# Issuing a gated recurrence and its projections in a written order on one Trainium2 core

## The chip, the cores and the metric

The kernel runs on one core of one Trainium2 chip. A core has a tensor engine (PE, matrix products and transposes), a vector engine (DVE), a scalar engine (ACT, activations and copies), GpSimd (POOL) and a sync engine (SP) that issues most DMAs. Each engine works through its own list of instructions in the order of that list, and engines wait for each other by semaphores. The metric is the device time of one execution in microseconds.

## The reference

One step of a streaming encoder with one layer: 512 prompt frames and 32 frames of a running stream, model width 2048, all in float32. Half of the token mixer is latent attention, half is a gated linear recurrence (HGRN2) with 8 heads of 128 features. The stage that is changed computes the recurrence:

```python
proj = x @ w_in
hq, hf, hi, hg, cq, ckv, kr = jnp.split(proj, SPLITS, axis=-1)
f = lb + (1.0 - lb) * jax.nn.sigmoid(hf)
# S_t = diag(f_t) S_{t-1} + k_t outer v_t (k_t = 1 - f_t), o_t = S_t^T q_t
o_h, s_new = hgrn2_recurrence(heads(hq), heads(1.0 - f), heads(jnp.log(f)), heads(hi), s0, blk)
o_h = rms_norm(o_h, hgrn_norm_g) * jax.nn.silu(hg)
...
out = jnp.concatenate([o_h, o_a], axis=-1) @ w_out
```

Behind it come a normalisation, a convolutional feed-forward network and a last normalisation.

## The kernel before

Activations lie with features on the 128 partitions and all 544 frames along the free axis. Each float32 operand of a large product is split into a high part (`wh` of a weight, `aH` of an activation, rounded by ACT) and a low part (`wl`, `aL`: what the rounding left, subtracted by DVE), and a product is three matmuls: high by high, high by low, low by high.

**The projections of heads 2 to 7** are made by one step of Strassen's scheme over halves of the frames and of the input features. A *group* makes two projections of a head, `divided_qf(h)` the query q and the forget gate f, `divided_ig(h)` the value i and the output gate g. Each group is seven *products*, in the order 11, s1, s2, s4, s3, 12, 22. A product is 24 matmuls with 272 columns, eight blocks of features by three (L753). Its weight is a quarter matrix of 128x1024 or a difference of quarters: `form` (L711, DVE) makes the difference for s1, s2, s3 and 22, `split` (L717 on ACT, L718 on DVE) makes wh and wl. Products 11, 12 and s4 take a loaded quarter as it is; `form("11")` issues the four loads of a group. When a product ends, its result is copied by ACT (L759) or added by DVE (L762) into the projection's tile `hproj`, and the gate's function follows (sigmoid on ACT; L774 or L784 on DVE).

**The recurrence of a head** runs beside these products. `levels(h)` has nine steps: Kp = 1 - f and Qp = q*f (L801, L802); the diagonal term (dps, L807) with level 1; levels 2, 4, 8, 16, 32, 64, each with four or five small matmuls of Kp by Qp (L822, L824, L827), an update of Qp on DVE (L828), one of Kp on POOL (L830), and a masked copy of the scores into `attnT` (L840); at last a record of the tiles. Each level's matmuls read Kp and Qp as the level before left them. `finish(h)` makes the head's outputs: transposes of Kp and of the value (L856) into one PSUM tile `sw`, copied by ACT to kT (L858, L859) and vT (L861); the state products (L866) and the states S on DVE (L871, L873); the output matmuls (L888, L890); their square on ACT (L893); its sum and a scaling on DVE (L896, L897); a power on POOL (L898); the product with it on DVE (L900); the transposes of that (L906), again in `sw`; and the scaling by the gate (L908, L910).

**The order.** `weave` lets the levels of head h run beside `divided_ig(h)`, and the outputs of head h beside `divided_qf(h+1)`, by a ratio of steps. This only sets priorities: the scheduler that builds each engine's list chooses among what it holds to be ready. `ready(n + 2)` has the weights of the product two ahead formed and split. Elsewhere the kernel uses `tc.manual_schedule(engines=MANUAL)`, under which PE, DVE and ACT get their instructions in the order in which the code issues them; POOL and SP stay with the scheduler. Behind the last group `out_first` runs the outputs of head 7 beside the first products with `w_out`, whose operands are split at L176 and L177.

Of the kernel before, what the change touches and what calls it, by code (L numbers as in the profile page):

```python
# [7 lines left out]
F32 = mybir.dt.float32  # L8
# [3 lines left out]
ALU = mybir.AluOpType  # L12
# [3 lines left out]
P = 128  # L16
# [43 lines left out]
def tile_encoder_step(ctx, tc, xp, xs, w_in, w_in4, w_kr, w_q_b, w_kv_b, w_out, w_up, w_gate, w_down, w_down2,  # L60
# [579 lines left out]
    with tc.tile_pool(name="gp", bufs=1) as gp, tc.tile_pool(name="psg", bufs=1, space=PSUM) as psg:  # L640
# [49 lines left out]
        class Divided:  # L690
# [19 lines left out]
                    if n == name:  # L710
                        V.tensor_tensor(out=r[out], in0=r[a], in1=r[b], op=ALU.subtract)  # L711

            def split(self, name):
                key = {"11": "11", "12": "21", "s1": "11", "s2": "11", "s3": "12", "s4": "22", "22": "21"}[name]
                wh = wp.tile([P, 1024], R, name="wh", tag="wh")
                wl = wp.tile([P, 1024], R, name="wl", tag="wl")
                A.activation(wh, self.raw[key], AF.Copy)  # L717
                V.tensor_tensor(out=wl, in0=self.raw[key], in1=wh.bitcast(F32), op=ALU.subtract)  # L718
                return wh, wl

        def operand(name, k):
# [6 lines left out]
        split_of, begun = {}, []  # L728

        def ready(n):  # L730

            if not begun:
                products[0][0].form(products[0][1])
            while len(begun) <= min(n, len(products) - 1):
                m = len(begun)
                split_of[m] = products[m][0].split(products[m][1])
                begun.append(m)
                if m + 1 < len(products):
                    products[m + 1][0].form(products[m + 1][1])

        def divided(c, a, b, after):
            ps = main_tile()
            x, y = ps[:, :NI], ps[:, 512:512 + NI]
            t0, t1 = H_
            for i, name in enumerate(ORDER):
                n = 7 * (c - N_PLAIN) + i
                ready(n + 2)
                wh, wl = split_of.pop(n)
                out = x if name in ("11", "s2", "s3", "22") else y
                for k in range(HK):  # L750
                    oh, ol = operand(name, k)
                    for q, (ww, aa) in enumerate(((wh, oh), (wh, ol), (wl, oh))):
                        PE.matmul(out, ww[:, k * P:(k + 1) * P], aa, start=name in ("11", "s1", "12") and k == 0 and q == 0,  # L753
                                  stop=k == HK - 1 and q == 2, skip_group_check=True)
                    if k % 4 == 3:
                        yield
                kept = {"11": a[:, t0], "s1": b[:, t1], "s2": b[:, t0], "22": a[:, t1]}.get(name)
                if kept is not None:
                    A.activation(kept, out, AF.Copy)  # L759
                else:  # L760
                    z = {"s4": b[:, t0], "s3": b[:, t1], "12": a[:, t0]}[name]
                    V.tensor_tensor(out=z, in0=z, in1=out, op=ALU.add)  # L762
                    if name != "12":
                        after(z)

        def proj_tile():
            return hp.tile([P, T], F32, name="hproj", tag="hproj")

        def divided_qf(h):
            q, f = proj_tile(), proj_tile()  # L770
# [5 lines left out]
            hq[h], hf[h] = q, f  # L776

        def divided_ig(h):
            i, g = proj_tile(), proj_tile()

            def gate(z):
                e = gp.tile([P, 2, NI], F32, name="sg", tag="sg")[:, 0]
                A.activation(e, z, AF.Sigmoid)
                V.tensor_tensor(out=z, in0=z, in1=e, op=ALU.mult)  # L784
            yield from divided(2 * h + 1, i, g, gate)
            hi[h], hgate[h] = i, g

        def sw_tile():
            return psg.tile([P, 1024], F32, name="sw", tag="sw")
# [59 lines left out]
        def finish(h):  # L849
            v, gate = hi[h], hgate[h]  # L850
            Kp, Qp, tot, tots, at, s0 = rec[h]
            vT = gp.tile([P, 5, P], F32, name="vT", tag="vT", bufs=1)
            for src, dst in ((Kp, kT), (v, vT)):
                tp = sw_tile()
                for j, (a, b) in enumerate(TOK):
                    PE.transpose(tp[:, j * P:(j + 1) * P], src[:, a:b], ident)  # L856
                if dst is kT:
                    A.activation(kT[:, :4].rearrange("p j c -> p (j c)"), tp[:, :512], AF.Copy)  # L858
                    A.activation(kT[96:128, 4], tp[96:128, 512:640], AF.Copy)  # L859
                else:  # L860
                    A.activation(dst.rearrange("p j c -> p (j c)"), tp[:, :640], AF.Copy)  # L861
                yield
            yield
            ss = s1_tile()
            for c in range(4):
                PE.matmul(ss[:, c * P:(c + 1) * P], kT[:, c], vT[:, c], start=True, stop=True)  # L866
            S = [None]
            for c in range(4):
                sc = gp.tile([P, P], F32, name="S", tag="S", bufs=4)
                if c == 0:  # L870
                    V.tensor_copy(sc, ss[:, 0:P])  # L871
                else:
                    V.scalar_tensor_tensor(out=sc, in0=S[c], scalar=tot[:, c:c + 1], in1=ss[:, c * P:(c + 1) * P],  # L873
                                           op0=ALU.mult, op1=ALU.add)
                S.append(sc)
            dma(stp_d[h], S[4])
            ss = s1_tile()
            PE.matmul(ss[:, :P], kT[:, 4], vT[:, 4], start=True, stop=True)
            s1o = gp.tile([P, P], F32, name="s1o", tag="s1o", bufs=1)
            V.scalar_tensor_tensor(out=s1o, in0=s0, scalar=tots[:, 16:17], in1=ss[:, :P], op0=ALU.mult, op1=ALU.add)  # L880
            dma(sts_d[h], s1o)
            yield
            yield
            ops_ = sw_tile()
            for c, (ta, tb) in enumerate(TOK):
                cs = slice(c * P, (c + 1) * P)
                st = S[c] if c < 4 else s0
                PE.matmul(ops_[:, cs], at[:, ta:tb], vT[:, c], start=True, stop=c == 0)  # L888
                if c:
                    PE.matmul(ops_[:, cs], Qp[:, ta:tb], st, start=False, stop=True)  # L890
            o3 = ops_[:, :640].rearrange("p (c v) -> p c v", c=5)
            sq = gp.tile([P, 5, P], F32, name="sqg", tag="sqg", bufs=1)
            A.activation(sq, o3, AF.Square)  # L893
            r0 = gp.tile([P, 5], F32, name="r0", tag="r0", bufs=2)
            r1 = gp.tile([P, 5], F32, name="r1", tag="r1", bufs=2)
            V.reduce_sum(out=r0, in_=sq, axis=AX.X)  # L896
            V.tensor_scalar(out=r0, in0=r0, scalar1=1.0 / P, scalar2=RMS_EPS, op0=ALU.mult, op1=ALU.add)  # L897
            G.tensor_tensor(out=r1, in0=r0, in1=nhalf, op=ALU.pow)  # L898
            on = sq
            V.tensor_tensor(out=on, in0=o3, in1=r1[:, :, None].to_broadcast([P, 5, P]), op=ALU.mult)  # L900
            yield
            yield
            yield
            tp = sw_tile()
            for c in range(5):
                PE.transpose(tp[:, c * P:(c + 1) * P], on[:, c], ident)  # L906
# [18 lines left out]
        weave([beside(head_ig(1), of_inputs, 2)], [levels(1), finish(0)], 1.2)  # L925
        run(of_inputs)
        place_s3()
        weave([divided_qf(2)], [finish(1)], 0.8)
        for h in range(2, HEADS):
            weave([divided_ig(h)], [levels(h)], 0.7)  # L930
            if h < HEADS - 1:
                weave([divided_qf(h + 1)], [finish(h)], 0.8)
        wo_tiles = [main_tile(), main_tile()]

        def out_first():
            for kk in range(4):
# [5 lines left out]
            fin = finish(HEADS - 1)  # L942
            ks = CAT_ORDER
            for kk in range(4):
                wh, wl = out_piece(ks[kk * 4] // 4, 0)
# [1258 lines left out]
```

## Time and profile before

| | us |
|---|---|
| median of 3 runs | 2438.55 (2436.04 to 2440.56) |
| the profiled execution, device time | 2439.59 |
| its span in the profile | 2437.8 |
| the groups of heads 2 to 7, first to last matmul of L753 | 380.8 to 765.2 |
| mean granted clock of PE over the span | 0.987 |

The page gives the busy time of each engine and the groups of instructions. The stage in question is about a sixth of the span. It is best read by head: the same work repeats six times there, so rows for equal stretches can be compared.

### The profile page before, as it was taken

The page shows a single profiled execution, that of the slowest core. Times are in us where ns is not written, and L with a number is a line of the kernel's source. Part 1 is how long each engine was busy: PE and PEld are TensorE (multiplying, and loading weights), DVE is VectorE, ACT ScalarE, POOL GpSimd, SP SyncE. Part 2 cuts the span into 40 slices and gives each one's busy share as a digit, 9 for nine tenths or more (in the row PEclk, how much of TensorE's full clock was granted, in tenths as well). Part 3 has the DMA queues.
Part 4 walks back from the last instruction along what each step waited for, and adds up shares of the span by engine and source line. Part 5 has one row for each costly group of instructions (what it writes and reads, how often), then busy time and mean ns, then how long its engine had stood idle before and what let it go on. Part 6 is the DMA issues. An engine that isn't in the chain of part 4 may idle for free.

```text
span 2437.8 us, 44485 instructions
## 1 busy us (share of the span) xinstructions
PE 2356.3 (97%) x18462; PEld 2324.2 (95%) x18462; DVE 1801.7 (74%) x2459; ACT 1037.5 (43%) x1603; POOL 188.6 (8%) x219
## 2 busy tenths in 40 slices
PE   6999999999999999999999999999999999999997
PEld 6999898989889999989999999999999999999996
DVE  7445577666666546889888888888877888888566
ACT  4244433333333224655555555455444433333234
POOL 4010021111111110000000000000000100000023
PEclk9999999999999999999999999999999999999998
DMA  7232263222225433735444353535343874632312
GB/s 231 93 93 70 62 202 101 73 78 76 72 66 187 138 106 110 224 112 178 159 158 147 130 175 111 194 103 180 102 126 111 338 300 150 232 133 88 123 62 74
DMA packets 131913, 333.20 MB, mean 137 GB/s; under 512 B 11904, under 2 KB 64896, under 8 KB 127104
## 3 DMA queue, kind: packets, MB, share of 16 engines
q1 hardware_dynamic: 122448, 286.91, 36.0%
q0 software_dynamic: 5040, 39.00, 4.0%
q10 hardware_dynamic: 4224, 4.46, 0.5%
q8 instruction: 145, 2.38, 0.4%
q14 instruction: 56, 0.46, 0.1%
HBM read 272.78 MB, written 56.15 MB: 135 GB/s over the span
## 4 chain that ended last, share of the span: by engine, by line
PE 64%; DVE 3%; ACT 1%; issue 1%; ACTq 0%; DVEq 0%
PE main L1179 20%; PE acc L1179 16%; PE main L1207 8%; PE main L118 7%; PE acc L1207 6%; PE acc L118 5%; DVE wl L1131 1%; PE main L753 1%; ACT zb L1299 0%; ACT wh L1130 0%; DVE raw L1123 0%; DVE ops L1260 0%; DVE zb L1294 0%; DVE wl L107 0%; PE main L993 0%
## 5 line engine op out<-in xcount | busy, mean ns | idle before, releaser
L1130 ACT ACTIVATE wh<-raw 128x1024 fp32r<-128x1024 f32 x340 | 359.9, 1059 | 415.6 <-DVE raw L1123 133.2
L1131 DVE TENSOR_TENSOR wl<-raw,wh 128x1024 fp32r<-128x1024 f32 x340 | 415.8, 1223 | 134.7 <-ACT wh L1130 133.8
L1179 PE MATMUL main<-op,wh 128*128 128x272 f32 x1408 | 265.7, 288 | 0.0
L1179 PE MATMUL acc<-ops,wh 128*128 128x272 f32 x1344 | 256.6, 289 | 4.2 <-DVE ops L1260 4.2
L1179 PE MATMUL main<-ops,wh 128*128 128x272 f32 x1344 | 254.2, 287 | 0.0
L1179 PEld LDWEIGHTS main<-op,wh 128*128 128x128 f32 x1408 | 221.0, 188 | 0.0
L1179 PEld LDWEIGHTS acc<-ops,wh 128*128 128x128 f32 x1344 | 212.9, 190 | 4.4 <-DVE ops L1260 4.4
L1179 PEld LDWEIGHTS main<-ops,wh 128*128 128x128 f32 x1344 | 211.0, 188 | 0.0
L1179 PE MATMUL main<-op,wl 128*128 128x272 f32 x704 | 203.1, 289 | 0.9 <-DVE wl L1131 0.9
L1179 PE MATMUL acc<-ops,wl 128*128 128x272 f32 x672 | 194.7, 290 | 0.0
L1179 PE MATMUL main<-ops,wl 128*128 128x272 f32 x672 | 193.8, 288 | 0.2 <-DVE wl L1131 0.2
L118 PE MATMUL main<-aH,wh 128*128 128x272 f32 (+2 forms) x768 | 183.5, 296 | 1.5 <-ACT x L267 1.5
L118 PE MATMUL main<-aL,wh 128*128 128x272 f32 (+2 forms) x768 | 180.2, 292 | 4.0 <-POOL aL L269 3.9
L118 PE MATMUL main<-aH,wl 128*128 128x272 f32 (+2 forms) x768 | 179.0, 291 | 0.0
L717 ACT ACTIVATE wh<-raw 128x1024 fp32r<-128x1024 f32 x84 | 88.9, 1059 | 193.0 <-PE main L753 85.5
L107 DVE TENSOR_TENSOR wl<-raw,wh 128x1024 fp32r<-128x1024 f32 (+2 forms) x80 | 89.8, 1127 | 103.8 <-ACT wh L106 98.7
L1179 PE MATMUL acc<-op,wh 128*128 128x272 f32 x832 | 157.7, 288 | 1.6 <-DVE eg L1403 1.6
L1130 ACT ACTIVATE wh<-rawl 128x1024 fp32r<-128x1024 f32 x93 | 98.5, 1060 | 105.9 <-DVE rawl L1123 41.8
L1123 DVE TENSOR_TENSOR raw<-raw,raw 128x1024 f32<-128x1024 f32 x114 | 139.2, 1221 | 1.7
L106 ACT ACTIVATE wh<-raw 128x1024 fp32r<-128x1024 f32 (+2 forms) x80 | 75.5, 950 | 147.8 <-PE acc L118 65.6
L1131 DVE TENSOR_TENSOR wl<-rawl,wh 128x1024 fp32r<-128x1024 f32 x93 | 113.8, 1223 | 32.7 <-ACT wh L1130 32.6
L118 PEld LDWEIGHTS main<-aL,wh 128*128 128x128 f32 x768 | 129.9, 191 | 4.9 <-POOL aL L269 4.9
(421 smaller groups left out, 6189.6 us busy)
## 6 DMA issues: line engine op xcount, KB each, us to landing
raw<-in_w_in SPq DMA_DIRECT2D x76, 512.0 KB, 3.6
raw<-in_w_up SPq DMA_DIRECT2D x72, 512.0 KB, 4.6
raw<-in_w_gate SPq DMA_DIRECT2D x72, 512.0 KB, 3.8
raw<-in_w_down SPq DMA_DIRECT2D x71, 512.0 KB, 4.0
raw<-in_w_out SPq DMA_DIRECT2D x40, 512.0 KB, 3.6
opd<-ohl SPq DMA_DIRECT2D x16, 1088.0 KB, 5.5
ops<-opd POOLq DMA_DIRECT2D x16, 1088.0 KB, 9.6
opd<-ohl SPq DMA_DIRECT2D x16, 816.0 KB, 6.4
```

What stands on the lines that cost most here:

```text
L106: A.activation(dst(hv), src(rv), AF.Copy)
L107: V.tensor_tensor(out=dst(lv), in0=src(rv), in1=dst(hv).bitcast(F32), op=ALU.subtract)
L118: PE.matmul(ps, ww[:, wcols[0]:wcols[1]], aa[:, hs[j]], start=first and i == 0, stop=last and i == 2, skip_group_check=True)
L717: A.activation(wh, self.raw[key], AF.Copy)
L753: PE.matmul(out, ww[:, k * P:(k + 1) * P], aa, start=name in ("11", "s1", "12") and k == 0 and q == 0, stop=k == HK - 1 and q == 2, skip_g ...
L1123: V.tensor_tensor(out=out, in0=a, in1=b, op=ALU.subtract)
L1130: A.activation(wh, src, AF.Copy)
L1131: V.tensor_tensor(out=wl, in0=src, in1=wh.bitcast(F32), op=ALU.subtract)
L1179: PE.matmul(ps, ww[:, k * P:(k + 1) * P], aa, start=self.first and k == 0 and i == 0, stop=k == n - 1 and i == 2, skip_group_check=True)
L1207: PE.matmul(banks[:, 512 * u:512 * u + NI], ww[:, (u * n + k) * P:(u * n + k + 1) * P], aa, start=self.first and k == 0 and i == 0, stop=k ...
```

## The change

The whole stage of heads 2 to 7 is put under `tc.manual_schedule`. The parts:

- `split` is divided into `high` (ACT, called by `begin` when a product starts, for the product two ahead) and `low` (DVE, called by `complete` when that product is half issued, followed by the `form` of the product three ahead).
- `divided` yields after each half product (12 matmuls). What takes a product's result is put on a list `later` and issued by `settle` in the middle of the next product. The gate's last multiplication goes through that list once more.
- Half products are the slots of one count, 28 to a head. Levels of head h start at slot 16 of the head (the middle of the second product of `divided_ig`) and take a step every 1.75 slots, every 1.375 for head 7; the outputs start 15 slots later and take one step a slot. So they run over the next two groups.
- `finish` has its yields moved: two behind each set of transposes, one between the square and its sum, one between the power and the product with it. It has eleven steps as before.
- The forget gate's multiply-add goes from DVE (L774) to ACT.

```diff
+        def begin(n):
+            if n < len(products):
+                ws_of[n] = products[n][0].high(products[n][1])
+
+        def complete(n):
+            if n < len(products):
+                ws_of[n] = products[n][0].low(ws_of[n])
+                if n + 1 < len(products):
+                    products[n + 1][0].form(products[n + 1][1])
+
+        def settle():
+            now, later[:] = later[:], []
+            for f in now:
+                f()
...
+            for i, name in enumerate(ORDER):
+                n = 7 * (c - N_PLAIN) + i
+                begin(n + 2)
+                wh, wl = ws_of.pop(n)
+                out = x if name in ("11", "s2", "s3", "22") else y
+                for k in range(HK):
+                    oh, ol = operand(name, k)
+                    for q, (ww, aa) in enumerate(((wh, oh), (wh, ol), (wl, oh))):
+                        PE.matmul(out, ww[:, k * P:(k + 1) * P], aa, start=name in ("11", "s1", "12") and k == 0 and q == 0,
+                                  stop=k == HK - 1 and q == 2, skip_group_check=True)
+                    if k == 3:
+                        settle()
+                        complete(n + 2)
+                        yield
+                later.append(lambda name=name, out=out: take(name, out))
+                yield
...
                 A.activation(z, z, AF.Sigmoid)
-                V.tensor_scalar(out=z, in0=z, scalar1=oml[:, h:h + 1], scalar2=lb[:, h:h + 1], op0=ALU.mult, op1=ALU.add)
+                A.activation(z, z, AF.Identity, bias=lb[:, h:h + 1], scale=oml[:, h:h + 1])
...
             A.activation(sq, o3, AF.Square)
+            yield
             r0 = gp.tile([P, 5], F32, name="r0", tag="r0", bufs=2)
...
             G.tensor_tensor(out=r1, in0=r0, in1=nhalf, op=ALU.pow)
+            yield
             on = sq
             V.tensor_tensor(out=on, in0=o3, in1=r1[:, :, None].to_broadcast([P, 5, P]), op=ALU.mult)
-            yield
             yield
             yield
...
-        weave([divided_qf(2)], [finish(1)], 0.8)
-        for h in range(2, HEADS):
-            weave([divided_ig(h)], [levels(h)], 0.7)
-            if h < HEADS - 1:
-                weave([divided_qf(h + 1)], [finish(h)], 0.8)
...
+        with tc.manual_schedule(engines=MANUAL):
...
+            def beside_from(slot, gen, steps, pace):
+                for n in range(steps):
+                    turns.setdefault(slot + int(n * pace), []).append(gen)
+
+            beside_from(0, finish(1), 11, 1)
+            for h in range(2, HEADS):
+                s0 = 28 * (h - 2) + 16
+                beside_from(s0, levels(h), 9, 1.75 if h < HEADS - 1 else 1.375)
+                if h < HEADS - 1:
+                    beside_from(s0 + 15, finish(h), 11, 1)
+            groups = [g for h in range(2, HEADS) for g in (divided_qf(h), divided_ig(h))]
+            for slot, _ in enumerate(s for g in groups for s in g):
+                for gen in turns.pop(slot, ()):
+                    next(gen, None)
```

What this does to the engines' lists shows in three places. In the rows, `L753` of before is `L773` of the change, `L824` and `L827` are `L838` and `L841`, `L856` is `L870`.

First, DVE beside the outputs of head 2, in the group q, f of head 3. `wl` are splits (L718, in the change L721), L711 forms, L762 (L761) adds of results; `r` is the sum of squares (L896, in the change L911) and its scaling, `sqg` the product with the power. Before:

```order
L762 TENSOR_TENSOR hproj<-hproj,main 128x272
L718 TENSOR_TENSOR wl<-raw,wh 128x1024
L896 TENSOR_REDUCE r_5068<-sqg 128x5
L774 TENSOR_SCALAR hproj<-hproj,oml,lb 128x272
L897 TENSOR_SCALAR r_5068<-r_5068 128x5
L711 TENSOR_TENSOR raw<-raw 128x1024
L900 TENSOR_TENSOR sqg<-sw,r_5069 128x640
L762 TENSOR_TENSOR hproj<-hproj,main 128x272
```

In the change:

```order
L761 TENSOR_TENSOR hproj<-hproj,main 128x272
L721 TENSOR_TENSOR wl<-raw,wh 128x1024
L711 TENSOR_TENSOR raw<-raw 128x1024
L911 TENSOR_REDUCE r_5129<-sqg 128x5
L912 TENSOR_SCALAR r_5129<-r_5129 128x5
L916 TENSOR_TENSOR sqg<-sw,r_5130 128x640
L761 TENSOR_TENSOR hproj<-hproj,main 128x272
L721 TENSOR_TENSOR wl<-raw,wh 128x1024
L711 TENSOR_TENSOR raw<-raw 128x1024
L923 SCALAR_TENSOR_TENSOR og<-sw,par,hproj 128x512
L925 SCALAR_TENSOR_TENSOR og<-sw,par,hproj 128x32
L721 TENSOR_TENSOR wl<-raw,wh 128x1024 x2
```

Behind these rows stand one more form (L711) and the Kp of head 3 (L815). The form now stands ahead of the sum of squares; the product with the power follows the scaling at once. ACT's list at the same place in the change, where L907 is the square, L716 the high part of a weight, L789 and L790 the forget gate:

```order
L716 ACTIVATE wh<-raw_4782 128x1024
L789 ACTIVATE hproj<-hproj 128x272
L790 ACTIVATE hproj<-hproj,lb,oml 128x272
L907 ACTIVATE sqg<-sw 128x640
L716 ACTIVATE wh<-raw 128x1024
```

The last row is the weight of the next group's product 11, whose `wl` is the second row of DVE's list above; it comes behind the square.

Second, PE at two levels of head 3. Before (the level's scores are `s_5288`, the next level's `s_5311`):

```order
L753 MATMUL main<-s_3428,wl 128x272
L824 MATMUL s_5288<-Qp,Kp 128x64 x4
L827 MATMUL s_5288<-Qp,Kp 128x16
L824 MATMUL s_5311<-Qp,Kp 128x64 x3
L753 MATMUL main<-s_3429,wh 128x272 x2
```

In the change:

```order
L773 MATMUL main<-s_3430,wl 128x272
L838 MATMUL s_5302<-Qp,Kp 128x64 x4
L841 MATMUL s_5302<-Qp,Kp 128x16
L773 MATMUL main<-s_3431,wh 128x272 x2
L773 MATMUL main<-s_3431,wl 128x272
```

Before, a level followed the one before it at once; now a whole product of 24 matmuls lies between them.

Third, PE behind the last group, where the transposes of head 7 for its outputs meet the first matmuls of `w_out` (L118). Before:

```order
L856 MATMUL sw<-ident,Kp 128x128 x5
L118 MATMUL main<-aH,wh 128x272 x2
L118 MATMUL main<-aL,wh 128x272 x2
L118 MATMUL main<-aH,wl 128x272 x2
L118 MATMUL main<-aH,wh 128x272 x2
L118 MATMUL main<-aL,wh 128x272 x2
L118 MATMUL main<-aH,wl 128x272 x2
L856 MATMUL sw<-ident,hproj 128x128 x5
```

In the change:

```order
L870 MATMUL sw<-ident,Kp 128x128
L118 MATMUL main<-aH,wh 128x272 x2
L118 MATMUL main<-aL,wh 128x272 x2
L870 MATMUL sw<-ident,hproj 128x128 x5
L880 MATMUL s_8040<-vT,kT 128x128 x4
L892 MATMUL s_8054<-vT,kT 128x128
L902 MATMUL sw<-vT,attnT_3422 128x128
L118 MATMUL main<-aH,wl 128x272 x2
```

Twelve matmuls of `w_out` stood between the two sets of transposes and now four do; before, 24 more stood ahead of the state products, and now none.

More of the change, by code (lines that the diff above doesn't have):

```diff
@@ L711, in form, with high, low @@
                         V.tensor_tensor(out=r[out], in0=r[a], in1=r[b], op=ALU.subtract)
[L713 to L714 removed]
+            def high(self, name):
+                self.src = self.raw[{"11": "11", "12": "21", "s1": "11", "s2": "11", "s3": "12", "s4": "22", "22": "21"}[name]]
                 wh = wp.tile([P, 1024], R, name="wh", tag="wh")
+                A.activation(wh, self.src, AF.Copy)
+                return wh
+            def low(self, wh):
                 wl = wp.tile([P, 1024], R, name="wl", tag="wl")
[L717 to L718 removed]
+                V.tensor_tensor(out=wl, in0=self.src, in1=wh.bitcast(F32), op=ALU.subtract)
                 return wh, wl
@@ L727, in tile_encoder_step @@
         products = [(g, name) for g in map(Divided, range(N_PLAIN, 2 * HEADS)) for name in ORDER]
[L728 to L739, printed above, removed]
+        ws_of, later = {}, []
+        def begin(n):
[10 more added lines that the diff above has]
+                f()
         def divided(c, a, b, after):
@@ L744, in divided, with take @@
             t0, t1 = H_
[L745 to L755, printed above, removed]
-                        yield
+            def take(name, out):
                 kept = {"11": a[:, t0], "s1": b[:, t1], "s2": b[:, t0], "22": a[:, t1]}.get(name)
@@ L783, in gate @@
                 A.activation(e, z, AF.Sigmoid)
-                V.tensor_tensor(out=z, in0=z, in1=e, op=ALU.mult)
+                later.append(lambda: V.tensor_tensor(out=z, in0=z, in1=e, op=ALU.mult))
             yield from divided(2 * h + 1, i, g, gate)
-            hi[h], hgate[h] = i, g
         def sw_tile():
@@ L927, in tile_encoder_step @@
         place_s3()
-        weave([divided_qf(2)], [finish(1)], 0.8)
-        for h in range(2, HEADS):
-            weave([divided_ig(h)], [levels(h)], 0.7)
-            if h < HEADS - 1:
-                weave([divided_qf(h + 1)], [finish(h)], 0.8)
+        products[0][0].form("11")
+        for n in range(2):
+            begin(n)
+            complete(n)
+        last_finish = finish(HEADS - 1)
+        with tc.manual_schedule(engines=MANUAL):
+            turns = {}
+            def beside_from(slot, gen, steps, pace):
[11 more added lines that the diff above has]
+                    next(gen, None)
+            for _ in range(2):
+                settle()
+            for slot in sorted(turns):
+                for gen in turns[slot]:
+                    next(gen, None)
         wo_tiles = [main_tile(), main_tile()]
```

10 lines of the change are left out of this document (4 added, 6 removed).

## The prediction

> **What bounds the kernel now.** I read the page first, then busy time and granted clock by head, then the tensor engine's waits in the stage.
>
> ```profile
> PE 2356.3 (97%) x18462; PEld 2324.2 (95%) x18462; DVE 1801.7 (74%) x2459; ACT 1037.5 (43%) x1603; POOL 188.6 (8%) x219
> ```
>
> The tensor engine (PE) is the bound. A change that only orders the work of one stage can win what PE loses in that stage, and no more. The stage runs from 385 to 767 us; one row is one head, from its outputs' first transposes to those of the next (us, PE busy, PEld, DVE, ACT, POOL, granted clock, DMA share, GB/s):
>
> ```profile
> 385.00:447.10 62.10, 57.31 (x455) 55.67 (x455) 42.99 (x66) 21.03 (x32) 8.45 (x8) 1.00 0.24 77
> 447.10:512.20 65.10, 60.36 (x455) 58.72 (x455) 42.95 (x65) 21.00 (x32) 8.45 (x8) 0.95 0.24 73
> 512.20:575.90 63.70, 58.82 (x455) 57.17 (x455) 42.98 (x65) 21.14 (x33) 8.45 (x8) 0.97 0.24 74
> 575.90:638.00 62.10, 57.34 (x455) 55.70 (x455) 42.97 (x65) 21.08 (x33) 8.46 (x8) 1.00 0.25 77
> 638.00:703.10 65.10, 60.36 (x455) 58.71 (x455) 42.98 (x65) 20.98 (x32) 8.44 (x8) 0.95 0.24 72
> 703.10:767.10 64.00, 59.50 (x450) 58.09 (x451) 44.04 (x73) 27.21 (x46) 8.46 (x8) 0.95 0.42 139
> ```
>
> Two losses show. At full clock PE is busy 57.3 of 62.1 us, so it idles about 4.8 us a head. And four heads of the same work take 3.0, 1.6, 3.0 and 1.9 us more, 9.5 in all, at a granted clock under 1. The idle time has four causes (PE's waits, 340 to 800 us: total, times, longest):
>
> ```profile
> PE s L824 <- POOL Kp L830: 7.9, 13, 1.1
> PE sw L856 <- ACT kT L859: 7.4, 6, 1.2
> PE s L824 <- DVE attnT L840: 7.0, 6, 1.2
> PE sw L906 <- DVE sqg L900: 6.7, 7, 1.1
> ```
>
> They sum to 29.0 us. Never does PE wait for split weights (wh, wl). The lost clock is tied to the idle time (PE busy, count, granted clock):
>
> ```profile
> 481.51:484.92 3.41, 2.25 (x20) 1.00 0.00 0
> 484.92:488.33 3.41, 3.41 (x17) 0.50 0.20 43
> ...
> 614.60:618.02 3.42, 2.33 (x21) 1.00 0.49 153
> ```
>
> After 3.41 us with 2.25 busy, the next 3.41 us run at half clock; after 2.33 busy near 618 they do not. A clock of 0.95 over 65.1 us is two such stretches, 0.97 one: seven in the stage, 9.5 us, so I price one at 1.5 us.
>
> [...]
>
> **What the change removes.** (1) The wait for kT (7.4). Between a head's two sets of transposes PE now has 24 matmuls instead of 12. (2) Most of the waits for Kp and attnT (14.9). Levels that stood back to back are now 24 half-product matmuls apart, sometimes 12. What must fit into the space:
>
> ```profile
> 461.81 0.29 PE L753 MATMUL main<-aL,wh 128*128 128x272 f32 x1
> ...
> 462.56 0.29 PE L753 MATMUL main<-aL,wh 128*128 128x272 f32 x1
> L830 POOL TENSOR_TENSOR Kp<-Kp,tot 128x272 f32<-128x272 f32 (+1 forms) x35 | 31.0, 886 | 103.2 <-PE s L827 68.6 <-issue 23.3 <-DVE wl L718 8.9
> 446.14 1.06 ACT L717 ACTIVATE wh<-raw 128x1024 fp32r<-128x1024 f32 x1 [0.93 <-PE main L753]
> 447.10 0.58 ACT L858 ACTIVATE kT<-sw 128x512 f32<-128x512 f32 x1
> 447.69 0.27 ACT L859 ACTIVATE kT<-sw 32x128 f32<-32x128 f32 x1
> ```
>
> Six matmul starts lie in 0.75 us: 0.125 each, so 12 are 1.5 and 24 are 3.0 us. Kp's 0.89 us on POOL with its handovers fits into 1.5, and the two kT copies (0.85) behind one 1.06 us split fit into 3.0.
>
> **What it adds: the output's normalisation.** ACT, DVE and PE now obey the written order. In the change's lists the square of a head's output (ACT) stands ahead of the split wh of the next group's product "11"; DVE has wl of that product and the following form ahead of the sum of squares; and the output's last transposes stand 48 matmuls behind its matmuls. Today's chain, and today's prices:
>
> ```profile
> 461.08 0.39 PE L890 MATMUL sw<-s,Qp 128*128 128x128 f32 x2
> 461.22 0.37 PE L753 MATMUL main<-aH,wh 128*128 128x272 f32 x1
> 461.60 0.69 ACT L893 ACTIVATE sqg<-sw 128x640 f32<-128x640 f32 x1
> 462.55 0.81 DVE L896 TENSOR_REDUCE r<-sqg 128x5 f32<-128x640 f32 x1
> 463.60 0.17 DVE L897 TENSOR_SCALAR r<-r 128x5 f32<-128x5 f32 x1
> 463.85 2.07 POOL L898 TENSOR_TENSOR r<-r,nhalf 128x5 f32<-128x5 f32 x1 [22.41 <-DVE r L897]
> 465.95 0.82 DVE L900 TENSOR_TENSOR sqg<-sw,r 128x640 f32<-128x640 f32 x1 [1.06 <-POOL r L898]
> 466.69 0.43 DVE L762 TENSOR_TENSOR hproj<-hproj,main 128x272 f32<-128x272 f32 x1
> 466.83 0.55 PE L906 MATMUL sw<-ident,sqg 128*128 128x128 f32 x3 [1.08 <-DVE sqg L900]
> L717 ACT ACTIVATE wh<-raw 128x1024 fp32r<-128x1024 f32 x84 | 88.9, 1059 | 193.0 <-PE main L753 85.5 <-issue 61.4 <-DVE raw L711 42.7
> L718 DVE TENSOR_TENSOR wl<-raw,wh 128x1024 fp32r<-128x1024 f32 x84 | 102.5, 1221 | 31.7 <-ACT wh L717 31.1
> L711 DVE TENSOR_TENSOR raw<-raw 128x1024 f32<-128x1024 f32 x36 | 46.4, 1289 | 0.2
> 453.62 1.22 DVE L718 TENSOR_TENSOR wl<-raw,wh 128x1024 fp32r<-128x1024 f32 x1
> 454.75 0.34 DVE L873 SCALAR_TENSOR_TENSOR S<-S,totk,s 128x128 f32<-128x128 f32 x1
> ```
>
> A queued DVE instruction starts 0.08 to 0.09 us before its predecessor ends (453.62 to 454.75 for 1.22); ACT's likewise (446.14 to 447.10). Let t be the end of the output matmuls (461.47 today). The square starts at t+0.13; wh at t+0.73, ending t+1.79; wl at t+1.82; the form at t+2.95; the sum of squares at t+4.09 and its small scaling until t+5.11; POOL's power from t+5.19 to t+7.26; the product with it until t+8.11; PE can transpose at t+8.17. PE itself gets there sooner: its next matmul starts 0.25 before t (461.22), and 48 of them, 6.0 us, with about 0.15 for the switch end at t+5.9. So PE waits **2.2 us** where it waited 1.08. This holds for the outputs of heads 2 to 6: **11.0 us**. Head 1's outputs start on the other half of a product; there the sum of squares stands ahead of the split and nothing waits.
>
> **The next head's first level is late in turn.** Behind that product with the power DVE has, in the change's list: an add (0.43), wl, a form, the output's scaling, wl, wl, a form, then Kp.
>
> ```profile
> L801 DVE TENSOR_SCALAR Kp<-hproj 128x544 f32<-128x544 f32 x7 | 3.1, 437 | 0.0
> ```
>
> With X the start of the transposes, the add starts at X-0.14, wl at X+0.21, the form at X+1.35, ending X+2.57. Only then can ACT make the next wh (1.06, until X+3.67) and DVE its wl at X+3.71. The following wh ends at X+4.93 and its wl starts at X+4.97, the next form at X+6.11, Kp runs from X+7.25 to X+7.69. PE arrives after the transposes and 48 matmuls, 0.65+6.0, at about X+6.7: it waits **1.0 us**, five times (heads 3 to 7), **5.0 us**. In head 2, without the first delay, Kp is done 0.4 us early. The later levels come out with 0.6 us or more to spare.
>
> **The stage's end.** The last head's outputs are issued behind the ordered region. Before, 12 and 24 filler matmuls stood behind the two sets of transposes; now 4 and none:
>
> ```profile
> 450.48 0.70 ACT L861 ACTIVATE vT<-sw 128x640 f32<-128x640 f32 x1 [2.09 <-PE sw L856]
> 765.73 0.71 PE L856 MATMUL sw<-ident,Kp 128*128 128x128 f32 x5
> 767.97 0.77 PE L856 MATMUL sw<-ident,hproj 128*128 128x128 f32 x5
> 771.58 0.61 PE L866 MATMUL s<-vT,kT 128*128 128x128 f32 x4
> ```
>
> The 1.5 us between 766.44 and 767.97 were just filled; 8 fewer matmuls leave 1.0 open. The copy of vT (0.70 and a handover) now lies open too: 0.8. Together **1.8 us**.
>
> **No cost:** the forget gate's multiply-add moves from DVE to ACT, where 21 of 62 us are busy, and the product needs it only a group later; the weight loads keep their order but for one. I see no row for a price of the issue order itself, so I bound it from -1 us (12 switches of operand kind a head instead of 13, some 0.15 each) to +1 and take 0.
>
> **Sum.** Idle 29.0 goes, 11.0+5.0+1.8 = 17.8 comes: -11.2. Clock: eleven gaps of 1 to 2.2 us can each bring none or one half-clock stretch, 0 to 16.5 us; of today's gaps about a third to a half do so, and a stretch before a level hides part of the wait for Kp. I take 4, 6.0 us, against 9.5 now: -3.5. The sum is -14.7 us. The profiled execution took 2439.59 (span 2437.8), 1.0 above the median 2438.55; so 2424.9 there and **2424** as a median.
>
> **Rivals.** (a) Fixed order removes nearly all idle time: if DVE's wl and form before the sum of squares run earlier than I think (were wh ready before the square), the chain from t shortens by wh, wl and form less their overlaps, some 3 us, and both new waits vanish: -29.0-9.5, **2400**. Against it: the ACT list puts the square first, and ACT does not overtake. (b) Every new gap costs a stretch: 17.8+16.5 = 34.3 against 38.5, **2434**, no change to speak of. For it: the gap before the transposes is twice today's, and Kp's sits before two levels back to back, where half clock starts today; against it: the lone gaps of 1.1 to 1.2 before transposes do not halve the clock in the two heads at 1.00. (c) Slower: DVE becomes the bound. It is busy 43.0 us a head; its waits for ACT between a form and the following wl (eight a head, about 1.1) and for the power (2.1) bring 54, still under PE's 57.3. The 25 or so instructions a head that read PE's results, now in fixed places, would have to cost 0.45 us of waiting each to pass 65 us a head, today's slowest; at 0.55 a head takes 67.8, some 4 us above today's mean of 63.7, and six heads make **2463**. Nothing shows waits of that size where DVE has 12 or 24 matmuls of slack, but the fixed order has not run.
>
> **Chances.** My forecast (2412 to 2432) 0.62, (a) 0.14, (b) 0.15, (c) 0.09. Differences below 0.2%, 4.9 us, a measurement of this kernel can hardly tell from none, so faster means under 2433.7. Faster 0.76, same 0.15, slower 0.09. The range 2408 to 2437 leaves out the far part of (a) and (c).
>
> **What would show it.** Right: no wait for kT outside the end; waits for the output's product of about 2.2 us five times; waits of about 1 us for Kp ahead of the dps matmuls, five times; the sum of squares starting 4 us behind the output matmuls; three to six half-clock stretches. Wrong: if waits for wl appear on PE, (c) was at work; if the product with the power comes before PE gets there, (a).

## The result and the profile after

The changed kernel takes 2453.13 us (median of 5 runs, 2451.98 to 2453.87) against 2438.55 us (5 runs beside them): ratio 1.0055, 95% interval 1.004 to 1.0071. It is slower, and the prediction of 2424 with a range of 2408 to 2437 was wrong in sign.

The tensor engine (PE) is still the bound, with as much busy time as before (2354.3 us, 2356.3 before), so the time has gone into its idle stretches. Its waits in the changed kernel from 340 to 830 us (for whom; total us, times, longest) are these:

```profile
PE main L773 <- DVE hproj L761: 22.6, 23, 2.5
PE main L773 <- ACT hproj L758: 17.9, 31, 1.0
...
PE sw L921 <- DVE sqg L916: 1.1, 1, 1.1
PE s L880 <- ACT vT L875: 0.8, 1, 0.8
PE sw L870 <- ACT kT L873: 0.6, 1, 0.6
```

The four waits of before are gone, as forecast: of 29.0 us one wait for kT and one for the output's product are left, at the stage's end. In their place stands a wait that the prediction doesn't have. The product matmuls (L773) wait 54 times, 40.5 us in all, for the *take* of the product before: the copy out of PSUM on ACT (L758) or the add on DVE (L761). One case, from the timeline of the changed kernel (start, duration, instruction; in brackets how long the engine idled and for whom):

```profile
447.74 0.29 PE L773 MATMUL main<-s,wl 128*128 128x272 f32 x1
...
448.06 0.40 ACT L758 ACTIVATE hproj<-main 128x272 f32<-128x272 f32 x1 [1.86 <-PE main L773]
448.51 0.52 PE L773 MATMUL main<-s,wh 128*128 128x272 f32 x2 [0.49 <-ACT hproj L758]
```

The last matmul of a first half product ends at 448.03; ACT's copy starts 0.03 later and takes 0.40; PE goes on 0.05 after its end. So a copy of the previous product waits for the first twelve matmuls of this one, and the other twelve wait for the copy: a round trip of half a microsecond in the middle of the product. Yet the two don't share a column: the copy reads one half of the tile `main` (x, from column 0, or y, from column 512), the matmuls add to the other. The semaphores of the built program say the same: in the change every take that a half product waits for waits itself for a matmul on the other half of its tile, and 53 half products stand right behind that matmul with nothing between.

Where the add stands behind something else in DVE's list, the round trip is longer. The longest ones are the delayed normalisation of a head's output that I had forecast, though at another place than I had said:

```profile
473.01 0.82 DVE L916 TENSOR_TENSOR sqg<-sw,r 128x640 f32<-128x640 f32 x1 [1.28 <-POOL r L913]
473.75 0.43 DVE L761 TENSOR_TENSOR hproj<-hproj,main 128x272 f32<-128x272 f32 x1
474.10 1.22 DVE L721 TENSOR_TENSOR wl<-raw,wh 128x1024 fp32r<-128x1024 f32 x1
474.24 0.40 PE L773 MATMUL main<-aH,wh 128*128 128x272 f32 x1 [2.50 <-DVE hproj L761]
```

There are five of these, one for each of heads 2 to 6, 12.5 us together. The other 49 waits are at most 0.97 and make 28.0 us.

By head (us, PE busy, PEld, DVE, ACT, POOL, granted clock, DMA share, GB/s), the middle four of the six heads of the changed kernel; the outer two have a clock of 1.00:

```profile
450.90:516.60 65.70, 57.98 (x457) 55.56 (x456) 44.80 (x63) 22.36 (x33) 8.80 (x8) 1.00 0.24 73
516.60:583.90 67.30, 59.58 (x457) 57.17 (x457) 44.63 (x63) 22.39 (x33) 8.81 (x8) 0.97 0.22 69
583.90:649.80 65.90, 58.19 (x458) 55.78 (x457) 44.79 (x63) 22.43 (x34) 8.80 (x8) 1.00 0.24 72
649.80:715.70 65.90, 58.17 (x445) 55.75 (x444) 44.62 (x63) 22.34 (x33) 8.75 (x8) 0.97 0.22 70
```

At full clock a head takes 65.7 to 65.9 us, where it took 62.10 before; PE idles 7.7 of them instead of 4.8. In these six heads the clock is down in two places only, against seven stretches before, though PE waits more. Both places come right behind a stretch that holds one of the waits of 2.5 us; the first (PE busy, count, granted clock):

```profile
537.92:541.33 3.41, 1.34 (x10) 1.00 0.00 0
541.33:544.74 3.41, 3.41 (x19) 0.54 0.01 5
```

The other three waits of 2.5 us and the round trips of 0.5 us, spread over the stage, brought none.

The account of the profiled executions, 2452.24 against 2439.59: the waits shown make 43 instead of 29, which is +14; about five half-clock stretches fewer at 1.5 each, -7.5; busy time per head up by 0.7 in six heads, +4. That leaves 2 of the 12.7 us without a place.

### The profile page after: what moved, and what is told of

It is laid out like the page before. It is cut to its first block, busy times and chain, and to the rows that moved or that the text cites. A ratio compares the mean times of both kernels' runs of the same rounds, so it can differ in the third digit from the quotient of the medians.

```text
span 2450.5 us, 44455 instructions
## 1 busy us (share of the span) xinstructions
PE 2354.3 (96%) x18462; PEld 2317.5 (95%) x18462; DVE 1812.1 (74%) x2447; ACT 1045.2 (43%) x1615; POOL 191.5 (8%) x219
## 4 chain that ended last, share of the span: by engine, by line
PE 75%; DVE 6%; ACT 2%; issue 2%; POOL 0%; DMA 0%; ACTq 0%; SPq 0%; DVEq 0%
PE main L1217 20%; PE acc L1217 16%; PE main L773 9%; PE main L1245 8%; PE main L118 7%; PE acc L1245 6%; PE acc L118 5%; PE s L838 1%; DVE wl L1169 1%; ACT hproj L758 1%; ACT wh L716 0%; DVE wl L721 0%; DVE hproj L761 0%; ACT zb L1337 0%; PE sw L902 0%
## 5 line engine op out<-in xcount | busy, mean ns | idle before, releaser
L1168 ACT ACTIVATE wh<-raw 128x1024 fp32r<-128x1024 f32 x340 | 359.9, 1059 | 415.0 <-DVE raw L1161 134.4
L118 PE MATMUL main<-aL,wh 128*128 128x272 f32 (+2 forms) x768 | 180.1, 292 | 4.6 <-POOL aL L269 4.6
L118 PE MATMUL main<-aH,wh 128*128 128x272 f32 (+2 forms) x768 | 183.4, 296 | 1.1 <-ACT x L267 0.7
L118 PE MATMUL main<-aH,wl 128*128 128x272 f32 (+2 forms) x768 | 178.9, 291 | 0.0
L773 PE MATMUL main<-aH,wh 128*128 128x272 f32 x384 | 118.2, 308 | 22.6 <-DVE hproj L761 22.6
L118 PEld LDWEIGHTS main<-aL,wh 128*128 128x128 f32 x768 | 129.6, 191 | 5.8 <-POOL aL L269 5.7
```

What stands on the lines that cost most here:

```text
L118: PE.matmul(ps, ww[:, wcols[0]:wcols[1]], aa[:, hs[j]], start=first and i == 0, stop=last and i == 2, skip_group_check=True)
L1168: A.activation(wh, src, AF.Copy)
```

## Experiments

**Theory T**: the program ties every reading of a half of a PSUM tile to the matmuls on the whole tile, so `settle` in the middle of a product makes a round trip there. **Rival R**: the fixed order is dear in itself, ACT and DVE come late with what stands in their lists (the prediction's rival c). Each ratio below is against runs of the kernel before on the same chip, with its 95% interval.

### Two tiles, the fixed order kept

```diff
-            ps = main_tile()
-            x, y = ps[:, :NI], ps[:, 512:512 + NI]
+            if not halves:
+                halves.extend((main_tile(), main_tile()))
+            x, y = (halves[(c + j) % 2][:, :NI] for j in range(2))
```

PSUM use doesn't grow: the pool has two such tiles in any case.

> The change kept whole, its fixed order too, but the two halves x and y of a group's result lie in two PSUM tiles of their own, which change roles from group to group, so that no half product can be tied to the reading of the other half. Theory T (in the changed kernel the reading of one half of the tile by the take waits for the half product that is just being added to the other half, and the next half product waits for the take: 40.5 us of waits for hproj in front of the products): these waits fall from 40.5 to under 3 us, and the waits that the prediction named come out: for the output's product with the power about 2.2 us five times, for Kp about 1 us five times. 2452 - 40.5 + 15 = 2427, 2420 to 2432. Rival R (the fixed order itself is dear, ACT and DVE come late with splits and reads): waits of the same sum for wh, wl or hproj, 2446 to 2454.

Measured: 2405.55 us, ratio 0.9863 (0.9847 to 0.9878). PE's waits from 340 to 800 us:

```profile
PE sw L924 <- DVE sqg L919: 7.5, 6, 1.3
PE sw L824 <- DVE Kp L818: 2.5, 5, 0.5
PE main L776 <- ACT hproj L761: 2.0, 5, 0.4
```

Of the 54 waits five of 0.4 us are left, and the two that the prediction named have come out, five times each, the first once more at the end. No product of the stage waits for wh or wl. R falls: the order is the same and the kernel is 47.6 us faster. T had the size too small (2427, and 2405.55 lies below its range): against the changed kernel the waits fell by 29 us (43 to 14 with the stage's end), the two half-clock stretches in the heads went (3), and busy time at full clock fell from about 58.1 to 56.1 us a head (12 in six heads), which T had not counted; what such busy time holds is told with before_two_tiles. The chain that I had laid out from the end t of the output matmuls stands here as forecast (t is 455.47; timeline of two_tiles):

```profile
455.08 0.39 PE L907 MATMUL sw<-s,Qp 128*128 128x128 f32 x2
455.50 0.71 ACT L910 ACTIVATE sqg<-sw 128x640 f32<-128x640 f32 x1 [1.92 <-PE sw L907]
456.10 1.05 ACT L716 ACTIVATE wh<-raw 128x1024 fp32r<-128x1024 f32 x1
457.18 1.23 DVE L721 TENSOR_TENSOR wl<-raw,wh 128x1024 fp32r<-128x1024 f32 x1 [3.23 <-ACT wh L716]
458.44 1.23 DVE L711 TENSOR_TENSOR raw<-raw 128x1024 f32<-128x1024 f32 x1
459.59 0.81 DVE L914 TENSOR_REDUCE r<-sqg 128x5 f32<-128x640 f32 x1
460.44 0.17 DVE L915 TENSOR_SCALAR r<-r 128x5 f32<-128x5 f32 x1
460.69 1.17 POOL L916 TENSOR_TENSOR r<-r,nhalf 128x5 f32<-128x5 f32 x1 [21.55 <-DVE r L915]
461.88 0.82 DVE L919 TENSOR_TENSOR sqg<-sw,r 128x640 f32<-128x640 f32 x1 [1.28 <-POOL r L916]
462.76 0.77 PE L924 MATMUL sw<-ident,sqg 128*128 128x128 f32 x5 [1.27 <-DVE sqg L919]
```

The sum of squares starts at t+4.12 (forecast t+4.09), POOL at t+5.22 (t+5.19). Only POOL's power is 1.17 instead of 2.07, and by that 0.90 the transposes start at t+7.29 instead of t+8.17 and PE waits 1.27 instead of 2.2.

### One tile, the take issued at a product's end

```diff
                     if k == 3:
-                        settle()
                         complete(n + 2)
                         yield
                 later.append(lambda name=name, out=out: take(name, out))
+                settle()
                 yield
```

> The change with one PSUM tile as it was, but the take of a product is issued behind its own last matmul instead of in the middle of the next one. T: the round trip stays, and only its place moves to the start of the next product. In the program as built 28 half products, instead of 39, then wait for a take with no other matmul between; 40.5 x 28/39 = 29 us of waits for hproj, which is 11 us less: 2441, 2435 to 2447. If the takes were only late in their queues (R), issuing them a half product earlier would take away most of the 40 us: under 2425.

Measured: 2453.63 us, ratio 1.0052 (1.0038 to 1.0065), no better than the change. Waits from 340 to 800 us:

```profile
PE main L773 <- DVE hproj L761: 29.8, 24, 2.6
PE main L773 <- ACT hproj L758: 7.4, 15, 0.5
```

Both theories missed. The waits fell from 54 to 39. T's sum had a wrong count in it: in the lists as built 53 half products of the change, not 39, stand right behind the matmul that their take waits for, and 29 here, so T should have given 22 us of waits. ACT's 15 waits are the bare round trip of 0.49 us. But DVE's 24 took 1.24 each, so the place of the add in DVE's list seems to count as well. To test that, wl and the next form were put behind the take.

```diff
                     if k == 3:
-                        complete(n + 2)
                         yield
                 later.append(lambda name=name, out=out: take(name, out))
                 settle()
+                complete(n + 2)
                 yield
```

> take_at_end, with the low part wl and the next form (DVE) issued behind the take at a product's end instead of in its middle. In take_at_end the waits for ACT takes were 15 of 0.49 us, the bare round trip, but the 24 for DVE adds 1.24 us each. If the adds were dear because they stood in DVE's queue behind wl, form and a level's instructions, they now fall to about 0.5 to 0.7 us: 2453 - 24 x 0.6 = 2439, 2432 to 2444. If the 1.24 us is not a place in DVE's queue: 2450 to 2456.

Measured: 2429.81 us, ratio 0.9965 (0.9953 to 0.9978), 24 us less than take_at_end; the forecast range was left at the lower end.

```profile
PE main L773 <- DVE hproj L761: 10.7, 14, 2.6
PE main L773 <- ACT hproj L758: 8.0, 15, 1.1
```

The adds' waits fell from 29.8 to 10.7 us, and ten of them went altogether. So a tie costs the round trip plus whatever stands ahead of the reader in its list. T explains the tie; a part of R's lateness sits on top of it, and only because of it: in two_tiles, with the change's lists, PE waits for no add.

### One tile, the steps moved to where the tie is

```diff
-                beside_from(s0, levels(h), 9, 1.75 if h < HEADS - 1 else 1.375)
+                beside_from(s0, levels(h), 9, 2 if h < HEADS - 1 else 1.375)
                 if h < HEADS - 1:
-                    beside_from(s0 + 15, finish(h), 11, 1)
+                    beside_from(s0 + 16, finish(h), 11, 1)
```

> The change with one tile and its fixed order, only the numbers of the table altered: levels 2 steps apart instead of 1.75, the outputs 16 steps behind the levels' start instead of 15. So the steps that hold matmuls of levels and outputs fall into the middle of a product, between its halves, where the tie lies. In the program as built 12 half products, instead of 39, then follow a take with nothing between; behind the others stand 5 to 11 short matmuls. T: waits for hproj fall from 40.5 to 12 to 20 us, 2452 - 25 = 2427, 2418 to 2436. If the lateness of ACT and DVE were the cause (R), covering does nothing: 2446 to 2456.

Measured: 2407.71 us, ratio 0.9864 (0.985 to 0.9878). The first two waits by size, from 340 to 800 us:

```profile
PE main L773 <- DVE hproj L761: 4.0, 8, 0.5
PE main L773 <- ACT hproj L758: 2.9, 6, 0.5
```

Two numbers of the table take the change from 0.55% slower to 1.4% faster than before; the time lies below T's range of 2418 to 2436. The waits fell to 6.9 us, below the 12 to 20 that T gave. In the lists as built 13 ties have nothing between, of the change's 53, and 14 waits show, each of about 0.5 us; where four or more short matmuls stand between, PE hardly ever waits. Not all of the 45 us is cover: the outputs' step by itself also takes away the jam on DVE, five waits of 2.5 us in the change, and two_tiles_outputs_later below shows what that is worth with two tiles.

### The kernel before with two tiles, and its control

The first kernel is the one before with the edit of two_tiles alone.

> The kernel before with the two halves in two PSUM tiles, nothing else. T: before, the scheduler already hid the tie (waits of the products for hproj are 1.2 + 1.2 us over the stage), so little is to be had: 2433 to 2440, within 0.2% of 2438.55. If two tiles are worth something by themselves, without the fixed order, it shows here: under 2430.

The control holds the same two tiles for the whole stage but keeps x and y of a group together:

```diff
-            ps = main_tile()
+            if not halves:
+                halves.extend((main_tile(), main_tile()))
+            ps = halves[c % 2]
             x, y = ps[:, :NI], ps[:, 512:512 + NI]
```

> Control: the kernel before, where the stage takes its two PSUM tiles once and holds them, as in before_two_tiles, but x and y of a group stay in one tile and the groups alternate between the two. T (what counts is that x and y have a tile each): no change, 2434 to 2443. If the gain of before_two_tiles came from holding the tiles instead of asking the pool for one in every group: 2385 to 2395.

Measured: before_two_tiles 2388.79 us, ratio 0.9789 (0.9775 to 0.9803); the control 2438.31 us, ratio 0.9995 (0.9985 to 1.0005). The forecast for the first was far off: two tiles are worth 50 us to the kernel before, and the control, whose time and waits are those of before, shows that it is the separation of x and y that is worth it. (The 1.2 and 1.2 us in that forecast are idle time ahead of weight loads, PEld; no product matmul of before waited for a take.) Waits from 340 to 800 us, before_two_tiles:

```profile
PE main L991 <- DVE n_e L1002: 1.2, 1, 1.2
PE s L827 <- POOL Kp L833: 0.7, 2, 0.5
PE s L825 <- DVE totk L839: 0.3, 1, 0.3
PE sw L909 <- DVE sqg L903: 0.2, 1, 0.2
```

and those of the control:

```profile
PE s L828 <- POOL Kp L834: 8.4, 14, 1.1
PE sw L860 <- ACT kT L863: 7.4, 6, 1.2
PE s L828 <- DVE attnT L844: 7.0, 6, 1.2
PE sw L910 <- DVE sqg L904: 6.7, 7, 1.1
```

So the four waits that the prediction started from were no trouble of levels and outputs as such: the waits had the names of Kp, kT, attnT and sqg, their cause was the shared tile. How the tile caused them is argued, not shown. In the lists of before as built no half product that waits for a take stands right behind the matmul that the take waits for; at least three other tensor instructions lie between. It seems that the scheduler knew the tie and spent levels and outputs as cover for it, so that they came where the tie was, not where their own inputs were ready, and waited there. That fits these lists and the waits' vanishing; it was not tried by itself.

Two heads of before_two_tiles, in the columns of the rows by head above:

```profile
441.79:497.29 55.50, 55.50 (x457) 55.19 (x456) 42.78 (x65) 21.20 (x32) 7.60 (x8) 1.00 0.29 85
497.29:552.79 55.50, 55.50 (x457) 55.21 (x456) 42.79 (x65) 21.19 (x32) 7.59 (x8) 1.00 0.27 85
```

PE is busy for the whole of 55.50 us at full clock: no idle time shows here that another order could win. A head of before at full clock had 57.31 us busy for 455 instructions, some 1.8 us a head more, 11 in the stage. Part of that seems to be stalls inside busy time. A matmul here is shown with 0.29 us while the next starts 0.125 after it, so a stall shorter than the difference never shows as idle, and a longer one shows too short: in the round trip shown first, 0.77 us lie between the starts, 0.64 more than usual, of which 0.49 shows as a wait. In before, 1.37 us lie between the starts of the last product matmul and of the output's transposes (465.46 and 466.83), 1.24 more than usual, of which 1.08 shows; 33 waits that each hide some 0.15 would make about 5 of the 11, an estimate. Another part can be the order of PE's list, which changes between products and other matmuls 144 times in the stage instead of 168; how much each makes was not told apart. 29.0 idle, 9.5 of lost clock and these 11 make 49.5; measured were 49.8 by the medians.

### Without the fixed order

The changed kernel with `manual_schedule` left away, first with one tile, then with two:

```diff
-        with tc.manual_schedule(engines=MANUAL):
+        if True:
```

> The same code in the same places, but the scheduler may reorder it as it could before the change. T: the scheduler sees the tie between take and next half product and puts levels or other matmuls between (in the program as built at least three), so the waits for hproj fall under 10 us; some waits for Kp, attnT and the output's product come back: 2426 to 2440. R agrees that it gets faster than 2446, so this run alone does not tell the two apart; it shows whether the new places of the instructions, without the fixed order, are worth anything beside the kernel before.

> The change with two tiles and without the fixed order. T: neither tie nor jam is left, PE idles no more in the stage than in before_two_tiles: 2385 to 2393. If the new places of the instructions cost something by themselves: 2397 to 2406.

Measured: 2400.97 us (ratio 0.9839, 0.9826 to 0.9853) and 2389.62 us (0.9789, 0.9776 to 0.9803). With one tile the scheduler puts at least three other instructions into each tie, and only 3.6 us of waits for the adds are left. The time is lower than T's 2426 to 2440, and the waits for Kp and attnT that T expected back did not come; the reason stays open, since the edits weren't taken apart. With two tiles and no fixed order the changed kernel equals before_two_tiles, as forecast: once the tie is gone, the rest of the change is worth nothing that can be measured.

### Two tiles, fixed order, outputs one step later; the forget gate

```diff
-                    beside_from(s0 + 15, finish(h), 11, 1)
+                    beside_from(s0 + 16, finish(h), 11, 1)
```

> two_tiles, with the outputs one step later (16 instead of 15), so that the sum of squares of an output stands ahead of the split and the form of the next group's product, as it does in head 1. T: the waits that are left in two_tiles, 7.5 us for the output's product and 2.5 us for Kp, are that jam on DVE: they go, 2405.5 - 8 = 2397, 2392 to 2400. If the 16 us between two_tiles and before_two_tiles are the price of the fixed order itself (switches of operands, no overtaking): 2402 to 2408.

Measured: 2393.83 us, ratio 0.9807 (0.9793 to 0.9821). The waits of two_tiles for the output's product and for the Kp of the next head are gone; from 340 to 800 us the largest are

```profile
PE main L1029 <- DVE n_e L1040: 1.2, 1, 1.2
PE sw L924 <- DVE sqg L919: 1.1, 1, 1.1
PE s L883 <- ACT vT L878: 1.0, 1, 1.0
PE sw L873 <- ACT kT L876: 0.9, 1, 0.9
```

of which the last three belong to the stage's end. The jam was the sum of squares behind wl and the form, as the prediction had it, and the forecast range of 2392 to 2400 holds; so most of the 16 us were not a price of the fixed order. In this kernel the forget gate's multiply-add was put back on DVE:

```diff
-                A.activation(z, z, AF.Identity, bias=lb[:, h:h + 1], scale=oml[:, h:h + 1])
+                V.tensor_scalar(out=z, in0=z, scalar1=oml[:, h:h + 1], scalar2=lb[:, h:h + 1], op0=ALU.mult, op1=ALU.add)
```

> two_tiles_outputs_later, with the forget gate's multiply-add put back from ACT to DVE, where it was before the change. The prediction gave this move no cost and no gain: 2390 to 2397, within 0.1% of 2393.8. If ACT or DVE is near its limit in the fixed order, this moves the time by more than 5 us.

Measured: 2392.29 us, ratio 0.9805 (0.9793 to 0.9818), the same within the intervals.

The fastest kernel is the one before with two tiles, 2388.79 us, 2.1% under it (free_two_tiles can't be told from it).

## Why the prediction was wrong

- **"I see no row for a price of the issue order itself, so I bound it from -1 us ... to +1 and take 0."** This is the step that failed. The order puts the take between the halves of the next product, and the tie makes a wait of it: 54 times, 40.5 us. Five of these waits, 12.5 us, are the delayed normalisation that the sum had as 11.0 under another name; the other 49, 28.0 us, it put at nothing, and they undo nearly all of the 29.0 that the change removes. The bound was set from switches of operands, the only price that I looked for. I had taken x and y as separate, since their columns are; the lists show which instruction a waiting one waits for, and whether the second half waits for the take could have been read there. The trace of before had a hint: the waits of ACT and DVE for products, but none of product matmuls for takes; in the lists other matmuls stand between.
- **What the change removes (29.0 us)**: right by name and size, 29.0 to 1.7 at the stage's end. The reason given, too little space between these steps, was not the root: in before_two_tiles the waits go without any more space written in.
- **The wait for the output's product (2.2 us five times)**: right as a mechanism, shown in two_tiles (1.3) and taken away in two_tiles_outputs_later. The term of POOL's power was mis-sized, 2.07 for 1.17. The 0.15 for a switch of operands was an estimate without a row; with it PE was to get to the transposes at t+5.9, and it got there at t+6.02 in two_tiles (1.27 ahead of 462.76). In the changed kernel the wait comes at another place: the add behind the product with the power holds up a half product first (2.50 us, five times). That the sizes are near is luck.
- **The wait for Kp (1.0 us five times)**: 0.5 five times in two_tiles; its chain starts at the same product. The changed kernel doesn't show it, since PE had waited before.
- **The stage's end (1.8)**: 0.6 for kT and 0.8 for vT, near.
- **The forget gate at no cost**: right.
- **The clock (four stretches instead of seven)**: two in the heads; right in direction. Idle time in a stretch of 3.41 us doesn't settle it alone: in the trace of before PE was busy 2.17 us from 573.65 to 577.06, less than in the prediction's row, and the next stretch, to 580.47, ran at a clock of 1.00. In the changed kernel the clock was down in two heads with no wait of PE above 2.51 us in the stage. What decides it these traces don't show; four was an estimate from how often a gap of before had brought a half-clock stretch.
- **"Can win what PE loses in that stage, and no more"**, 38.5 us: what PE loses was put too low by 11, which counts as busy, in part, by the estimate of about 5, because the profile shows a stall shorter than it was (0.49 of 0.64 us).
- **The rivals**: (c) had the sign, but by luck: its mechanism is another one. DVE's reads did not become late by themselves: with two tiles the same order of reads costs PE 2.0 us of waits. What (c) gave as a test, waits for wl on PE, did not come.

## What to carry to other kernels

Before fixing an order by hand, list for each instruction that will stand between two others what it waits for and what waits for it, with tiles and not columns as the unit: two results that are read at different times belong into two tiles. A wait is named after what came last, so where several small waits of different names stand in one stage, ask what made the scheduler put the work there, and take a suspected tie away before moving anything. A PE that is busy 92% of a head (57.31 of 62.10 us in before) can lose more than its idle 4.8 us tell: with two tiles the head took 55.50.

## What the runs showed of the hardware

POOL's power on 128x5 took 1.17 us in seven of the eight outputs of the changed kernel and 2.07 in six of the eight outputs of before. In all six a form had started on DVE 0.17 us ahead of it; the row of POOL is in the prediction, DVE's beside it is

```profile
463.68 1.22 DVE L711 TENSOR_TENSOR raw<-raw 128x1024 f32<-128x1024 f32 x1
```

The form ends at 464.90, and the power at 465.92, 1.02 later, about as if it had begun only then. In the changed kernel's order DVE has nothing to do meanwhile (it waits 1.28 us for POOL in the row shown). In before_two_tiles an add ran on DVE beside the power, and the power took 1.17:

```profile
457.79 0.43 DVE L765 TENSOR_TENSOR hproj<-hproj,main 128x272 f32<-128x272 f32 x1
...
457.96 1.17 POOL L901 TENSOR_TENSOR r<-r,nhalf 128x5 f32<-128x5 f32 x1 [22.35 <-DVE r L900]
```

So the power took 0.90 us longer (2.07 against 1.17) beside a form of 1.22 us than beside an add of 0.43 or with DVE idle. Whether that lies in the form's length, in its operands or in something else these rows don't tell apart. A duration taken from a trace can hold a neighbour's time, and it changed here when the order did.
